# Half-size first weight blocks, zero products ahead of them, and a second load queue at the head of a hybrid decoder kernel

## The chip, the cores and the metric

One Trainium2 chip, one core. The metric is device time in microseconds (us). The kernel's engines are TensorE (PE, with its weight loads PEld), VectorE (DVE), ScalarE (ACT), GpSimd (POOL), and the queue of SyncE (SP) that issues transfers; ACT can issue transfers too.

## The reference

Two layers over 1024 prompt tokens and 8 decode tokens with 1024 features, all in float32. The change touches only the head of layer 0: RMSNorm of the input, then the combined input projection, of which the first part computed is the value projection of the first gated-linear-attention head together with the low-rank gate code.

```
h = rmsnorm(x, norm_g[0])
q, k, v, g, a_low, hb, gate_b, gate_c, z_b = _split(h @ w_in, EVEN_SPLITS)
```

The RMS factor of a token is applied after the product, so the products begin on x times the norm's gain. Everything behind that (the linear attention, the short convolution, the output projection, the convolution module of layer 1, the last norm) is as it was.

## The kernel before

**Number format.** Each float32 operand is cut in two parts: a high part in the fast matmul format (an ACT copy) and a low part, operand minus high part (a DVE or POOL subtraction). A product of two operands is three matmuls: high by high, high by low, low by high. `split_ahead` (L228) cuts the weight blocks (tiles wh and wl from the raw block wr), `split_x` (L295) cuts the input (tile A; ACT at L296, DVE at L297), and it also multiplies by the norm's gain, which stands in the first eight columns of the parameter tile prm.

**Weights.** A list, `plan`, holds the weight blocks in the order of their use. `load_ahead` (L218) issues the transfer of a block into one of two raw buffers, `split_ahead` cuts it. The first two blocks are 128 x 1088 each and hold k = 0 to 3 and k = 4 to 7 of the first value projection.

**Input.** The first 128 tokens come in two tiles xf of four k each, at L307; the other tokens of chunk 0 (256 columns for each of eight k), then chunks 1 and 2, then the first 128 tokens again in the layout needed later, come through `load_x` (L300), 32 transfers in all. All of these, the two weight blocks and prm are issued from SP's queue, in the order weight block, prm, xf, weight block, xf, and then the 32.

**The first products.** `v_proj(0)` (L337) runs over nine token tiles t; for each it runs over k = 0 to 7 with three matmuls each (L351), 216 matmuls of up to 272 columns. Tile t = 0 needs the two xf tiles and both weight blocks; t = 1 and 2 need the rest of chunk 0.

**Order.** ACT's instructions, the transfers it issues among them, stay in the order of the program text (`manual_schedule`). The order on PE, DVE, POOL and SP is set by a planner that plays the program through in simulated time (`schedule_with_timeline_sim`); it also places every semaphore. ACT loads its function table ahead of its first activation. The small tile scT, zeroed on POOL at L330, is later the masked score tile of the attention.

Of the kernel before, what the change touches and what calls it, by code (L numbers as in the profile page):

```python
# [7 lines left out]
F32 = mybir.dt.float32  # L8
F32R = mybir.dt.float32r
I32 = mybir.dt.int32  # L10
AF = mybir.ActivationFunctionType
ALU = mybir.AluOpType
# [3 lines left out]
P = 128  # L16
# [21 lines left out]
NPAR = _o  # L38
# [23 lines left out]
def hybrid_step(ctx, tc, xT, wv, wa, wup, woa, wic, woc, par, ident_d, mask_d, smask_d, sgla, ssc, scc,  # L62
                y_o, glap_o, scp_o, ccp_o, glas_o, scs_o, ccs_o):
    nc = tc.nc
    pe, act, dve, pool, sp = nc.tensor, nc.scalar, nc.vector, nc.gpsimd, nc.sync
# [12 lines left out]
    def nm(s):  # L78
        cnt[0] += 1
        return f"{s}{cnt[0]}"  # L80

    def T(shape, dt=F32, s="t"):
        return ring.tile(shape, dt, tag="t", name=nm(s))
# [4 lines left out]
    def g_t():  # L88
        return gp.tile([P, 512], F32, tag="g", name=nm("g"))
# [8 lines left out]
    prm = const.tile([P, NPAR], F32, tag="prm", name="prm")  # L98
# [7 lines left out]
    def pcol(n, i):  # L106
        return prm[:, PAR[n] + i:PAR[n] + i + 1]
# [84 lines left out]
    raws, parts, used, sums_of = [], [], [0], {}  # L192
# [25 lines left out]
    def load_ahead(i):  # L218
        while len(raws) < min(i, len(plan)):
            _, src, n, e, _ = plan[len(raws)]  # L220
            if src is None:
                raws.append(None)
                continue
            raw = wp.tile([P, 1088], F32, tag="raw", name=nm("wr"), bufs=2)
            sp.dma_start(out=raw[:, :n], in_=src)
            raws.append(raw)

    def split_ahead(i):  # L228
        while len(parts) < min(i, len(plan)):
            load_ahead(len(parts) + 2)  # L230
            key, src, n, e, where = plan[len(parts)]
            raw = raws[len(parts)]
            if key[0] in ("s0", "s1"):
                raw = sums_of[key[1]][key[0] == "s1"]
            if where is ring:
                h, l = T([P, n], F32R, s="wh"), T([P, n], F32R, s="wl")
            else:
                h = wp.tile([P, 1088], F32R, tag="wh", name=nm("wh"))
                l = wp.tile([P, 1088], F32R, tag="wl", name=nm("wl"))
            act.activation(h[:, :n], raw[:, :n], AF.Copy)  # L240
            if isinstance(e, int):
                sp.dma_start(out=l[:, :n].bitcast(F32), in_=wl_d[e])
            else:
                e.tensor_tensor(out=l[:, :n], in0=raw[:, :n], in1=h[:, :n].bitcast(F32), op=ALU.subtract)  # L244
            parts.append((h, l))

    def pair_sums(q):
        if q not in sums_of:
            e0 = next(i for i, p in enumerate(plan) if p[0] == ("w0", q))
            load_ahead(e0 + 2)  # L250
            a, b = raws[e0], raws[e0 + 1]
            s0, s1 = T([P, KT * P], s="s0"), T([P, KT * P], s="s1")
            lo, hi = slice(0, 512), slice(512, 1024)
            dve.tensor_tensor(out=s0[:, lo], in0=b[:, lo], in1=b[:, hi], op=ALU.add)
            dve.tensor_tensor(out=s0[:, hi], in0=s0[:, lo], in1=a[:, lo], op=ALU.subtract)
            dve.tensor_tensor(out=s1[:, lo], in0=a[:, lo], in1=b[:, lo], op=ALU.subtract)
            dve.tensor_tensor(out=s1[:, hi], in0=a[:, hi], in1=s0[:, hi], op=ALU.subtract)
            sums_of[q] = s0, s1

    def W(*key, ahead=2):  # L260
        i = used[0]
        assert plan[i][0] == key, (plan[i][0], key)
        used[0] += 1
        split_ahead(i + 1 + ahead)
        return parts[i]
# [22 lines left out]
            tick()  # L288


    xk = [T([P, NT], s="x") for _ in range(KT)]
    xf = [T([P, 4, P], s="xf") for _ in range(2)]
    A = new_a("A")

    def split_x(c, k, src, lo, hi):  # L295
        act.activation(A[c][:, k, lo:hi], src, AF.Copy, scale=pcol("g0", k))  # L296
        dve.scalar_tensor_tensor(out=A[c][:, KT + k, lo:hi], in0=src, scalar=pcol("g0", k),  # L297
                                 in1=A[c][:, k, lo:hi].bitcast(F32), op0=ALU.mult, op1=ALU.subtract)

    def load_x(k, lo, hi):  # L300
        sp.dma_start(out=xk[k][:, lo:hi], in_=xT[:, k, lo:hi])

    load_ahead(1)
    sp.dma_start(out=prm, in_=par)
    for j in range(2):
        load_ahead(j + 1)
        sp.dma_start(out=xf[j], in_=xT[:, j * 4:j * 4 + 4, 0:P])  # L307
    parts_of = [(0, P, CH[0][1]), (1, 0, CH[1][1]), (2, 0, CH[2][1])]
    for c, lo, hi in parts_of:
        for k in range(KT):  # L310
            load_x(k, CH[c][0] + lo, CH[c][0] + hi)
    for k in range(KT):
        load_x(k, 0, P)
    for j in range(2):
        split_ahead(j + 1)
        for k in range(4):
            split_x(0, j * 4 + k, xf[j][:, k, :], 0, P)

    def split_rest():
        for c, lo, hi in parts_of:  # L320
# [5 lines left out]
    sp.dma_start(out=mask, in_=mask_d)  # L326
    smask = T([P, NT], s="smask")
    sp.dma_start(out=smask, in_=smask_d)
    scT = T([P, 2, 512], s="scT")
    pool.memset(scT, 0.0)  # L330
    al = T([P, 9, RS], s="al")
    pool.memset(al, 0.0)
    alT = T([RS, NT], F32R, s="alT")
# [3 lines left out]
    def v_proj(h):  # L337
        w, width = [W("v", h, j, ahead=2 - j if h else 1 - j) for j in range(2)], VW if h == 0 else DV
        V = [T([P, 4, DV], s="V") for _ in range(2)]
        for t in range(9):  # L340
            ps = mm_t()
            c = min(t // 3, 2)
            lo, m = t * P - CH[c][0], P if t < 8 else ND
            i = 0
            for k in range(KT):
                wh, wl = w[k // 4]
                ks = slice((k % 4) * width, (k % 4 + 1) * width)
                xh = A[c][:, k, lo:lo + m]
                xl = A[c][:, KT + k, lo:lo + m]
                for x, y in ((xh, wh), (xh, wl), (xl, wh)):  # L350
                    pe.matmul(ps[:m, :width], x, y[:, ks], start=(i == 0), stop=(i == 23))  # L351
                    i += 1
            e = act if h == 0 and t < V_ACT else dve
            copy = lambda out, in_: act.activation(out, in_, AF.Copy) if e is act else dve.tensor_copy(out, in_)
            if t < 8:
                copy(V[t // 4][:, t % 4, :], ps[:, :DV])
            else:
                vd = T([ND, DV], s="vd")
                copy(vd, ps[:ND, :DV])
            if h == 0:  # L360
                copy(al[:m, t, 0:RANK], ps[:m, DV:VW])
                if t in W_AT:
                    split_ahead(len(parts) + 1)
            tick()
        start(v_dec(h, vd))
        return V
# [432 lines left out]
    for i in range(KT):  # L799
# [3 lines left out]
        cuts = [slice(lo, lo + n) for lo, n in CH]  # L803
# [62 lines left out]
    for lo, n in CH:  # L866
        s = slice(lo, lo + n)
# [208 lines left out]
    for i in range(KT):  # L1076
# [28 lines left out]
        else:  # L1105
            for b, take in ((8 + i, take_gate), (i, take_u)):
                for c, s, ps in units(W("c", b), X):
# [4 lines left out]
                                 in1=pd[:, i, :], op0=ALU.mult, op1=ALU.add)  # L1112
# [237 lines left out]
```

## Time and profile before

| | us |
|---|---|
| median of three runs | 1295.73 |
| lowest, highest | 1295.63, 1297.95 |
| profiled execution | 1294.83 |
| its span, first to last instruction | 1293.1 |
| PE busy in it | 1257.2 (97%) |
| DVE, POOL, ACT busy | 842.5, 669.6, 578.2 |
| mean granted TensorE clock | 0.99 of full |

The busy times are of one profiled execution. "Idle before" is the time an engine stood still just before an instruction, with what released it. Rows of a timeline merge neighbouring instructions of one line: "x4" is four of them, and the second number is the time from the first one's start to the last one's end.

### The profile page before, as it was taken

The page shows a single profiled execution, that of the slowest core. Times are in us where ns is not written, and L with a number is a line of the kernel's source. Part 1 is how long each engine was busy: PE and PEld are TensorE (multiplying, and loading weights), DVE is VectorE, ACT ScalarE, POOL GpSimd, SP SyncE. Part 2 cuts the span into 40 slices and gives each one's busy share as a digit, 9 for nine tenths or more (in the row PEclk, how much of TensorE's full clock was granted, in tenths as well). Part 3 has the DMA queues.
Part 4 walks back from the last instruction along what each step waited for, and adds up shares of the span by engine and source line. Part 5 has one row for each costly group of instructions (what it writes and reads, how often), then busy time and mean ns, then how long its engine had stood idle before and what let it go on. Part 6 is the DMA issues. An engine that isn't in the chain of part 4 may idle for free.

```text
span 1293.1 us, 20369 instructions
## 1 busy us (share of the span) xinstructions
PE 1257.2 (97%) x8189; PEld 1236.5 (96%) x8189; DVE 842.5 (65%) x1150; ACT 578.2 (45%) x892; POOL 669.6 (52%) x405
## 2 busy tenths in 40 slices
PE   7999999999999999999999999997999999998995
PEld 7999999999999999999999999997999999997995
DVE  6542554445536999999976254216579899989636
ACT  7434616335345523333332233315666929548513
POOL 1455445538375555455645322312298989846313
PEclk9999999999999999999999999999999999999997
DMA  7113032242153432323249998732222323223203
GB/s 260 34 66 135 18 131 103 78 155 99 42 211 130 165 108 72 131 82 131 84 153 349 361 380 304 268 115 85 100 93 99 99 98 103 98 67 134 96 17 131
DMA packets 62542, 174.10 MB, mean 135 GB/s; under 512 B 7776, under 2 KB 25792, under 8 KB 62448
## 3 DMA queue, kind: packets, MB, share of 16 engines
q1 hardware_dynamic: 62176, 172.53, 37.9%
q8 instruction: 64, 1.05, 0.3%
q14 instruction: 30, 0.25, 0.1%
q10 hardware_dynamic: 272, 0.27, 0.1%
HBM read 128.37 MB, written 44.41 MB: 134 GB/s over the span
## 4 chain that ended last, share of the span: by engine, by line
PE 87%; DVE 6%; ACT 3%; POOL 2%; issue 1%; DMA 0%; DVEq 0%; ACTq 0%; POOLq 0%
PE mm L274 61%; PE mm L735 8%; PE mm L351 6%; PE g L735 6%; PE g L274 1%; PE g L552 1%; PE g L513 1%; DVE cv L1159 1%; PE g L579 1%; PE g L582 1%; PE g L514 1%; PE g L392 1%; DVE Y L1253 1%; DVE sqv L1146 0%; ACT L95 0%
## 5 line engine op out<-in xcount | busy, mean ns | idle before, releaser
L274 PE MATMUL mm<-A,wh 128*128 128x384 f32 (+1 forms) x1536 | 245.5, 311 | 0.0
L274 PEld LDWEIGHTS mm<-A,wh 128*128 128x128 f32 x1536 | 231.4, 188 | 0.8
L244 POOL TENSOR_TENSOR wl<-wr,wh 128x1024 fp32r<-128x1024 f32 x51 | 124.5, 2448 | 193.8 <-ACT wh L240 193.8
L274 PE MATMUL mm<-X,wh 128*128 128x384 f32 (+1 forms) x1152 | 195.8, 321 | 6.0 <-ACT wh L240 5.6
L274 PEld LDWEIGHTS mm<-X,wh 128*128 128x128 f32 x1152 | 184.4, 190 | 8.3 <-ACT wh L240 6.0
L240 ACT ACTIVATE wh<-wr 128x1024 fp32r<-128x1024 f32 (+1 forms) x104 | 109.0, 1055 | 139.2 <-PE g L735 51.1
L274 PE MATMUL mm<-A,wl 128*128 128x384 f32 (+1 forms) x768 | 129.6, 310 | 0.0
L274 PEld LDWEIGHTS mm<-A,wl 128*128 128x128 f32 x768 | 117.4, 188 | 0.1
L1027 POOL TENSOR_TENSOR pa<-pa,pr 128x1024 f32<-128x1024 f32 x45 | 110.4, 2454 | 12.8 <-ACT pr L1025 10.4
L351 PE MATMUL mm<-wh,A 128*128 128x256 f32 (+3 forms) x576 | 108.3, 287 | 6.4 <-ACT A L296 6.4
L1013 DVE SCALAR_TENSOR_TENSOR g<-u,late,g 128x512 f32<-128x512 f32 x150 | 102.3, 747 | 1.1 <-ACT g L1010 1.1
L274 PE MATMUL mm<-X,wl 128*128 128x384 f32 (+1 forms) x576 | 102.1, 318 | 0.0
L351 PEld LDWEIGHTS mm<-wh,A 128*128 128x128 f32 (+1 forms) x576 | 86.7, 180 | 8.3 <-ACT A L296 6.4
L274 PEld LDWEIGHTS mm<-X,wl 128*128 128x128 f32 x576 | 92.4, 188 | 0.1
L244 POOL TENSOR_TENSOR wl<-s,wh 128x1024 fp32r<-128x1024 f32 x24 | 67.9, 2840 | 41.1 <-ACT wh L240 41.1
L351 PE MATMUL mm<-wl,A 128*128 128x256 f32 (+3 forms) x288 | 82.2, 286 | 0.1
L274 PE MATMUL mm<-M,wh 128*128 128x384 f32 (+1 forms) x384 | 67.5, 328 | 3.4 <-ACT M L1175 2.3
L274 PEld LDWEIGHTS mm<-M,wh 128*128 128x128 f32 x384 | 63.1, 193 | 4.8 <-ACT M L1175 2.6
L986 DVE SCALAR_TENSOR_TENSOR g<-us,prm,g 128x512 f32<-128x512 f32 x70 | 52.8, 754 | 12.5 <-ACT g L984 10.9
L201 ACT ACTIVATE ph<-pw 128x1024 fp32r<-128x1024 f32 x27 | 28.5, 1057 | 66.9 <-DMA pw<-in_dram 34.0
L913 DVE TENSOR_TENSOR x<-mm,x 128x384 f32<-128x384 f32 (+1 forms) x21 | 10.7, 515 | 71.6 <-PE mm L274 46.4
L1025 ACT ACTIVATE pr<-u,late 128x512 f32<-128x512 f32 x90 | 57.2, 716 | 0.0
(287 smaller groups left out, 2581.5 us busy)
## 6 DMA issues: line engine op xcount, KB each, us to landing
wr<-in_dram SPq DMA_DIRECT2D x102, 512.0 KB, 3.4
pw<-in_dram SPq DMA_DIRECT2D x27, 512.0 KB, 6.8
wl_d<-pw SPq DMA_DIRECT2D x27, 512.0 KB, 5.1
wl<-wl_d SPq DMA_DIRECT2D x27, 512.0 KB, 3.6
b<-y_d SPq DMA_DIRECT2D x14, 516.0 KB, 7.4
bc<-dec_d SPq DMA_DIRECT2D x12, 512.0 KB, 5.0
O<-o_d SPq DMA_DIRECT2D x8, 768.0 KB, 9.9
x<-in_dram SPq DMA_DIRECT2D x8, 516.0 KB, 6.3
```

Of the source, the lines that this page charges most:

```text
L201: act.activation(h, r, AF.Copy)
L240: act.activation(h[:, :n], raw[:, :n], AF.Copy)
L244: e.tensor_tensor(out=l[:, :n], in0=raw[:, :n], in1=h[:, :n].bitcast(F32), op=ALU.subtract)
L274: pe.matmul(out, wl if p == "w" else wh, xl if p == "x" else xh, start=((first or into is None) and i == 0), stop=(part[1] and i == len(se ...
L351: pe.matmul(ps[:m, :width], x, y[:, ks], start=(i == 0), stop=(i == 23))
L392: pe.matmul(ps[:, :n], ones, t, start=(i == 0), stop=(i == len(terms) - 1))
L513: pe.matmul(ps[:, j * P:(j + 1) * P], ke[:, lo:lo + P], qe[:, lo:lo + P], start=True, stop=True)
L735: pe.matmul(out, (l if p == "w" else h)[:, ws], xs[k][p == "x"], start=(i == 0), stop=(i == 11))
L986: dve.scalar_tensor_tensor(out=cm if j == 15 else acc, in0=us[:, j:j + n], scalar=ev(j), in1=acc, op0=ALU.mult, op1=ALU.add)
L1013: dve.scalar_tensor_tensor(out=acc[r], in0=u[:, 1 - r, lo + j:hi + j], scalar=df(r, j), in1=acc[r], op0=ALU.mult, op1=ALU.add)
L1025: act.activation(pr[:, r, :], u[:, 1 - r, lo + j:hi + j], AF.Copy, scale=df(r, j))
L1027: pool.tensor_tensor(out=ac, in0=ac, in1=pr, op=ALU.add)
```

## The change

The first two weight blocks come in two transfers of half the columns each, and are cut in halves: high half, low half, then the two k of x that belong to it. SP issues the first xf tile ahead of the first weight block. prm moves to ACT's queue, in two transfers (its first eight columns, then the rest), and four of the eight transfers of chunk 0's rest (odd k) move to ACT's queue as well. All six stand at the head of ACT's program. scT and its zeroing move ahead, and three products of 256 columns on it go to a spare tile of PSUM that nothing reads.

```
             raw = wp.tile([P, 1088], F32, tag="raw", name=nm("wr"), bufs=2)
-            sp.dma_start(out=raw[:, :n], in_=src)
+            cuts = 2 if len(raws) < 2 else 1
+            for i in range(cuts):
+                cut = slice(i * n // cuts, (i + 1) * n // cuts)
+                sp.dma_start(out=raw[:, cut], in_=src[:, cut])
             raws.append(raw)
...
+            if len(parts) < 2:
+                for i in range(2):
+                    cut = slice(i * n // 2, (i + 1) * n // 2)
+                    act.activation(h[:, cut], raw[:, cut], AF.Copy)
+                    e.tensor_tensor(out=l[:, cut], in0=raw[:, cut], in1=h[:, cut].bitcast(F32), op=ALU.subtract)
+                    for k in range(2):
+                        k += i * 2
+                        split_x(0, len(parts) * 4 + k, xf[len(parts)][:, k, :], 0, P)
+                parts.append((h, l))
+                continue
...
+    scT = T([P, 2, 512], s="scT")
+    pool.memset(scT, 0.0)
+    idle = g_t()
+    for _ in range(3):
+        pe.matmul(idle[:, 0:256], scT[:, 0, 0:P], scT[:, 1, 0:256], start=True, stop=True)
...
     def load_x(k, lo, hi):
-        sp.dma_start(out=xk[k][:, lo:hi], in_=xT[:, k, lo:hi])
-
-    load_ahead(1)
-    sp.dma_start(out=prm, in_=par)
+        (act if lo == P and k % 2 else sp).dma_start(out=xk[k][:, lo:hi], in_=xT[:, k, lo:hi])
+
+    act.dma_start(out=prm[:, 0:8], in_=par[:, 0:8])
+    act.dma_start(out=prm[:, 8:NPAR], in_=par[:, 8:NPAR])
     for j in range(2):
+        sp.dma_start(out=xf[j], in_=xT[:, j * 4:j * 4 + 4, 0:P])
         load_ahead(j + 1)
-        sp.dma_start(out=xf[j], in_=xT[:, j * 4:j * 4 + 4, 0:P])
...
-    for j in range(2):
-        split_ahead(j + 1)
-        for k in range(4):
-            split_x(0, j * 4 + k, xf[j][:, k, :], 0, P)
+    split_ahead(2)
...
-    scT = T([P, 2, 512], s="scT")
-    pool.memset(scT, 0.0)
```

## Rows read from the trace of the kernel before

**Rows 1.** The page's first part: busy time, share of the span, instructions.
```profile
PE 1257.2 (97%) x8189; PEld 1236.5 (96%) x8189; DVE 842.5 (65%) x1150; ACT 578.2 (45%) x892; POOL 669.6 (52%) x405
```
**Rows 2.** PE's waits, whole span: us in total, times, longest.
```profile
PE mm L351 <- ACT A L296: 6.4, 1, 6.4
...
PE mm L274 <- ACT wh L240: 5.6, 1, 5.6
```
**Rows 3.** Windows, PE alone: length, busy (instructions), PEclk, DMA share, GB/s.
```profile
6.35:10.55 4.20, 4.06 (x15) 1.00 1.08 368
10.75:36.00 25.25, 25.25 (x204) 1.00 0.66 215
```
**Rows 4.** PE's timeline, end of the first tile's start: start us, us, line.
```profile
9.32 0.43 PE L351 MATMUL mm<-wl,A 128*128 128x272 f32 x1
9.55 0.65 PE L351 MATMUL mm<-wh,A 128*128 128x272 f32 x2
10.14 0.40 PE L351 MATMUL mm<-wl,A 128*128 128x272 f32 x1
...
10.61 0.29 PE L351 MATMUL mm<-wl,A 128*128 128x272 f32 x1
10.74 0.28 PE L351 MATMUL mm<-wh,A 128*128 128x272 f32 x1
```
**Rows 5.** ACT's timeline from the start, with idle time before and its releaser.
```profile
0.73 1.28 ACT L240 ACT_TABLE_LOAD   x1 [0.73 <-PEq L1328]
4.59 1.11 ACT L240 ACTIVATE wh<-wr 128x1088 fp32r<-128x1088 f32 x1 [2.58 <-DMA wr<-in_dram]
5.90 1.28 ACT L296 ACTIVATE A<-xf,prm 128x128 fp32r<-128x128 f32 x4 [0.20 <-DMA xf<-in_dram]
7.65 1.11 ACT L240 ACTIVATE wh<-wr 128x1088 fp32r<-128x1088 f32 x1 [0.47 <-DMA wr<-in_dram]
8.67 1.26 ACT L296 ACTIVATE A<-xf,prm 128x128 fp32r<-128x128 f32 x4
```
**Rows 6.** DVE's timeline of the same stretch.
```profile
6.94 1.14 DVE L297 SCALAR_TENSOR_TENSOR A<-xf,prm,A 128x128 fp32r<-128x128 f32 x4
8.79 1.29 DVE L244 TENSOR_TENSOR wl<-wr,wh 128x1088 fp32r<-128x1088 f32 x1 [0.71 <-ACT wh L240]
10.00 1.14 DVE L297 SCALAR_TENSOR_TENSOR A<-xf,prm,A 128x128 fp32r<-128x128 f32 x4
```
**Rows 7.** Transfers issued: queue, count, KB each, median us from issue to landing.
```profile
wr<-in_dram SPq DMA_DIRECT2D x2, 544.0 KB, 5.5
x<-in_dram SPq DMA_DIRECT2D x8, 128.0 KB, 5.1
xf<-in_dram SPq DMA_DIRECT2D x2, 256.0 KB
prm<-in_dram SPq DMA_DIRECT2D x1, 181.0 KB, 3.9
```
**Rows 8.** SP's timeline: issue start, length; the eleventh, twelfth and thirteenth transfer.
```profile
5.96 0.44 SPq L301 DMA_DIRECT2D x<-in_dram  x1
...
7.64 0.33 SPq L301 DMA_DIRECT2D x<-in_dram  x1
...
8.40 0.33 SPq L301 DMA_DIRECT2D x<-in_dram  x1
```
**Rows 9.** Windows: length, PE, PEld, DVE, ACT, POOL busy, PEclk, DMA share, GB/s.
```profile
3.00:4.00 1.00, 0.00 (x0) 0.00 (x0) 0.00 (x0) 0.00 (x0) 0.00 (x0) 1.00 0.98 390
...
7.00:8.00 1.00, 0.92 (x4) 0.92 (x5) 1.00 (x5) 0.53 (x2) 0.00 (x0) 1.00 1.09 343
```
**Rows 10.** ACT's queue, the one transfer that ACT issues in the kernel before.
```profile
1288.97 0.42 ACTq L1258 DMA_DIRECT2D out_dram<-Y  x1
```
**Rows 11.** POOL's timeline at the start: the zeroing of scT.
```profile
0.73 0.95 POOL L330 MEMSET scT<- 128x1024 f32 x1 [0.29 <-POOLq L1328]
```
**Rows 12.** The chain of waits: four plain float32 products of 256 columns, two records each.
```profile
106.00 1.73 PE g L552 x8
```

## The prediction, made before the changed kernel was run

> **What bounds the kernel now.** I read the page's busy times first: PE is busy for 97% of the span, no other engine for more than 65% [rows 1]. So the time moves only if PE's work starts earlier, runs faster or loses a gap. PE's waits, longest first, come next: the longest of all is the first one, 6.4 us, in which nothing has been multiplied yet [rows 2], and it is the only one that the change aims at. The stretch behind it shows what a shift there would be worth: from 10.75 to 36 us PE is busy for 25.25 us of 25.25 [rows 3], so whatever the first tile of the value projection gains or loses is passed on whole. What happens before 10.75 is therefore the question.
>
> PE's timeline there shows two things. The matmuls of 272 columns start 0.23 us apart (9.32, 9.55) and later 0.13 apart (10.61, 10.74) [rows 4]: 272 columns at 1.2 and at 2.4 GHz. Up to 10.55 there are 15 of them [rows 3], all at the low level. (The windows' column of the granted clock stays at 1.00 all the while [rows 3, 9]; the spacing is what I go by.) And at 10.14 the queue stands still for a moment: the two records from 9.55 are through at 10.0, and the next product needs the low part of the second weight block, which DVE cuts from 8.79 on, in 1.29 us [rows 4, 6]. So even a fast clock from the start would have met that wait; it would have saved the two slow matmuls behind it, 0.2 us. The chain that sets PE's progress is the second block's: landed at 7.65, ACT's copy, DVE's subtraction at 8.79, PE at 10.14.
>
> As a mark I take the start of the 25th matmul, where tile t = 0 is done: the 16th starts at 10.61 [rows 4], nine later at 0.125 us each is 11.74 us.
>
> **When transfers land.** With the sizes [rows 7] the landings of before lie on a line. The first block (544 KB) released ACT at 4.59. The transfers behind it are prm, xf, block two, xf, in one queue: 981 KB are in when the first xf releases ACT at 5.90, 1525 KB when the second block does at 7.65 [rows 5], and 1781 KB at the second xf. That last landing is read from the queue: SP's eleventh, twelfth and thirteenth transfers are issued at 5.96, 7.64 and 8.40 [rows 8], right behind the landings of the third (5.90) and fourth (7.65), so a transfer is issued only when the eighth before it is in, and the second xf, the fifth, landed at 8.4. From 544 to 1781 KB is 1237 KB in 3.81 us, 325 KB a us. So B KB in are reached at 2.92 + B/325 us; for 981 and 1525 KB this gives 5.94 and 7.61, as read. The 16 transfer engines are full in this time (share 0.98 and 1.09, 390 and 343 GB/s, with one queue) [rows 9].
>
> **Two queues.** Does a second queue bring its bytes beside the first or out of the same rate? With one queue the share stands at 1, so I take the same rate, shared equally while both have work. The trace has no stretch with two queues; the other end of the price is that SP's bytes are not delayed at all.
>
> The Trainium skill's page "DMA: Bandwidth & Descriptors", section "Issuing engines are not separate DMA queues", says that transfers issued from different engines run on the same 16 engines and interleave, and that a second issuer saves only issuing time. By that rule the change's second queue costs the first one bytes, as I take it; no run here shows two queues yet.
>
> **The sum.** SP now sends 256 (xf), 272, 272 (block one), 256, 272, 272 KB. ACT sends 181 KB of prm and 4 x 128 KB of x, 693 KB. In the kernel before, those 512 KB of x came behind everything that t = 0 needs; now they come ahead of its second half. Shared equally, block one's first half is in at 2 x 528 = 1056 KB, 6.17 us; its second half at 800 + 693 = 1493 KB, 7.51; the second xf at 8.30; block two's halves at 2021 and 2293 KB, 9.14 and 9.98, where the whole of it came at 7.65 before.
>
> ACT first issues six transfers at 0.42 us [rows 10], then loads its table, 1.28 us [rows 5]: ready at 0.73 + 2.5 + 1.28 = 4.5. With the eighth-before rule the last of the six may wait for prm (shared, 362 KB, 4.0 us), which makes it 5.7. Both are hidden by the landing at 6.17.
>
> Costs of the pieces, start to start: an ACT copy of 1088 columns 1.02 us (7.65 to 8.67), of 128 columns 0.30 [rows 5]; on a line, 544 columns 0.61. DVE: 1.21 for 1088 (8.79 to 10.00), 0.27 for 128 [rows 6]; 544 columns 0.68. So halves cost ACT 1.22 a block for 1.02, DVE 1.36 for 1.21. From block two's first half at 9.14: ACT's high half to 9.75, two k to 10.35, second high half (landed 9.98) to 10.96. DVE: low half 9.8 to 10.48, two k to 11.02, low half to 11.70, two k to 12.24. PE's last product of t = 0 starts at 12.28, the 25th at 12.41. That is 0.7 us later than 11.74.
>
> The clock does not change this. PE's first product comes at 6.17 + 0.61 + 0.30 + 0.04 = 7.1, and 24 at 0.227 end at 12.6; at the high level DVE sets 12.4. So the three products on zeros are worth 0 to 0.2 us here. They cost nothing: scT is zeroed at 1.68 [rows 11], a product of 256 columns takes 1.73/4 = 0.43 us at the high level [rows 12], twice that at the low, so they are done between 3.0 and 4.3, ahead of any data.
>
> Behind t = 0 nothing new is late: the rest of chunk 0 now lands with its total bytes unchanged (1781 + 8 x 128 = 2805 KB, 11.6 us), and ACT reaches it at 11.6 after its last two k. SP's queue is shorter by three issues, which no engine waits for at that point. So the sum is +0.7: 1295.5 for the profiled execution of 1294.83, and 1295.73 + 0.7 = 1296.4 beside the median, which lies 0.9 above that execution.
>
> **Rivals.**
>
> *The order wins.* If ACT's bytes do not hold up SP's, the landings are 4.54, 5.38, 6.17, 7.01 and 7.84. ACT is ready at 4.5, so block two's first half starts at 7.01: ACT's second high half ends at 8.83, DVE's last two k at 10.10, the 25th matmul starts at 10.27 at the high clock: -1.5, 1294.2. At the low clock PE starts at 5.5 and 24 x 0.227 ends at 10.95: -0.8. For it: the first xf and half a block are 528 KB where before 981 KB had to be in. Against it: the full share in rows 9.
>
> *ACT stands behind its own transfers.* ACT's order is that of the text, and its six transfers come before every activation. A transfer waits for the eighth before it. If the eight are counted in the order of the text over both queues, the last x on ACT waits for block two's second half, 7.84 to 9.98 us, and ACT's first copy starts 1.70 later (issue and table), at 9.5 to 11.7. Nothing is then missing, but ACT and DVE have the whole head to do: DVE 0.65 behind, four steps of 0.68 + 0.54, the 25th matmul at 15.2 to 17.4. That is +3.5 to +5.7, 1300.3 in the middle. It decides from the point at which ACT is held beyond 6.2 us. For it: the rows of SP show such holds. Against it: the two queues issue side by side in the planner's time, and if they are counted alternately the last x waits only for prm. No row shows how two queues are counted.
>
> *The order elsewhere.* The planner sets the order on four engines in simulated time, and scT and a PSUM tile are taken earlier. A different order later on can move the end by some microseconds either way, as the longest waits behind the head are of that size (the largest below the 6.4 is 5.6 us [rows 2]). Half that, 2.8: 1292.9 or 1298.5.
>
> *The change does nothing.* The terms cancel within 0.3: 1295.7. This lies between the first two cases.
>
> **Chances and range.** Forecast, with the cancelling case, 0.52; the order wins 0.24; ACT held 0.12; order elsewhere 0.12, both signs alike. The measurement can tell about 0.2% from no change, 2.6 us: 1293.1 to 1298.3. Faster than that needs the order elsewhere, or a gain beyond what I see: 0.10. Slower: ACT held, and half of the order elsewhere, less what stays inside: 0.16. The rest, 0.74, is within. The range from 1293.4 to 1299.5 holds the first two cases, the low edge of the third and most of the fourth; the likeliest case alone runs from 1295.7 to 1297.2.
>
> **What the profile would show.** The first product at about 7.1 us instead of 6.35, at 0.23 us spacing or 0.13. The second block's first half landing at about 9.1; at 7 the first rival is right. ACT's table load starting near 3.3 to 4.4 and not later; at 8 or later it is held. The matmuls of t = 0 spread with gaps for DVE's halves and the 25th start near 12.4. If PE ends the value projection of head 0 as early as before or earlier, the contention was mis-sized; if the time moves by over 3 us with the head in place, the cause lies elsewhere.

## The result, and the profile after

The changed kernel took 1304.91 us (median of 6 runs, 1303.56 to 1306.63) beside 1295.68 for the kernel before in the same session (6 runs, 1294.95 to 1297.95). The ratio is 1.0070, 95% interval 1.0058 to 1.0081: slower by about 9.1 us, where 1296.4 was forecast with a range up to 1299.5. The profiled executions agree: the span is 1301.8 us for 1293.1.

The busy line has hardly moved [rows 1]; PE is busy 3.4 us longer, 2.9 of them the zero products, and the span is 8.7 us longer. The loss is time in which PE computes none of the kernel's own products. (The profiled execution is the fastest of the six.)

```profile
PE 1260.6 (97%) x8195; PEld 1238.4 (95%) x8195; DVE 843.6 (65%) x1152; ACT 578.5 (44%) x894; POOL 668.9 (51%) x405
```

PE's waits of the first 110 us of the changed kernel (us in total, times, longest). The first answers to the first of [rows 2].

```profile
PE mm L365 <- ACT A L315: 6.8, 1, 6.8
PE mm L287 <- DVE la L510: 2.4, 1, 2.4
PE g L309 <- POOL scT L306: 1.7, 1, 1.7
...
```

ACT's timeline of the changed kernel at the start, the counterpart of [rows 5] (start, length, engine, line; the two rows behind the first "..." are the second and third of the four x transfers, read in windows of their own).

```profile
0.73 0.43 ACTq L322 DMA_DIRECT2D prm<-in_dram  x1
1.20 0.44 ACTq L323 DMA_DIRECT2D prm<-in_dram  x1
3.57 5.52 ACTq L320 DMA_DIRECT2D x<-in_dram  x4
9.12 1.28 ACT L246 ACT_TABLE_LOAD   x1 [9.12 <-DMA x<-in_dram]
10.42 0.66 ACT L246 ACTIVATE wh<-wr 128x544 fp32r<-128x544 f32 x1
...
5.07 0.33 ACTq L320 DMA_DIRECT2D x<-in_dram  x1
...
7.20 0.34 ACTq L320 DMA_DIRECT2D x<-in_dram  x1
...
12.69 5.32 ACT L315 ACTIVATE A<-x,prm 128x256 fp32r<-128x256 f32 x12
17.91 0.65 ACT L246 ACTIVATE wh<-wr 128x544 fp32r<-128x544 f32 x1
```

The four x are issued at 3.57, 5.07, 7.20 and 8.76 (the last 0.33 before 9.09), each held until an earlier transfer lands. ACT's table load, which was at 0.73, comes at 9.12, and its first copy at 10.42 where it was 4.59. The row of 17.91 shows something that I missed in the diff: the new `for i in range(2)` reuses the name of `split_ahead`'s argument, so the loop over blocks ends after the first one, and the second weight block is cut only behind twelve cuts of x.

How late PE is, at the same work, in the kernel before and then in the changed one: the first 256-column product of the second head, the column sums of the squared input, the last of the first three gate products (L458, L472), the first key and query products (L274, L287), the first score products (the changed kernel's fence also has its zero products and its two waits in the query and key products).

```profile
35.93 0.28 PE L351 MATMUL mm<-wl,A 128*128 128x256 f32 x1
...
47.73 1.90 PE L392 MATMUL g<-ss,ones 128*128 128x384 f32 x6
...
61.75 0.29 PE L458 MATMUL g<-alT,wup_r 80*128 80x264 f32 x1
...
65.16 2.96 PE L274 MATMUL mm<-A,wh 128*128 128x384 f32 x16
...
92.36 0.38 PE L513 MATMUL g<-E,tm 128*128 128x128 f32 x2
```

```profile
1.74 2.93 PE L309 MATMUL g<-scT 128*128 128x256 f32 x6 [1.74 <-POOL scT L306]
11.42 0.59 PE L365 MATMUL mm<-wh,A 128*128 128x272 f32 x1 [6.75 <-ACT A L315]
...
40.93 0.28 PE L365 MATMUL mm<-wl,A 128*128 128x256 f32 x1
...
55.63 1.90 PE L406 MATMUL g<-ss,ones 128*128 128x384 f32 x6
...
70.13 0.52 PE L287 MATMUL mm<-A,wh 128*128 128x384 f32 x2
70.49 0.28 PE L472 MATMUL g<-alT,wup_r 80*128 80x264 f32 x1
...
82.75 3.07 PE L287 MATMUL mm<-A,wh 128*128 128x384 f32 x16 [0.86 <-ACT wh L253]
88.19 4.50 PE L287 MATMUL mm<-A,wh 128*128 128x384 f32 x28 [2.36 <-DVE la L510]
...
100.98 0.38 PE L527 MATMUL g<-E,tm 128*128 128x128 f32 x2
```

PE starts 5.07 us later (11.42 for 6.35) and is 5.00 later at the second head (40.93 for 35.93) and still 4.97 later at the first key and query products (70.13 for 65.16). At the score products it is 8.62 later (100.98 for 92.36). So the loss has two terms: 5.0 in the head, and 3.6 between 70 and 101 us, of which two waits, 0.86 and 2.36, make 3.2. From there on it stays: the span ends 8.7 later. The column sums give a hint of the second term: they are 7.9 later while the products around them are 5.0 later, so they stand at another place in PE's order. The last of the first three gate products is 8.7 later (70.49 for 61.75).

### The profile page after: what moved, and what is told of

It reads as the page before. It is cut to its first block, busy times and chain, and to the rows that moved or that the text cites. A ratio compares the mean times of both kernels' runs of the same rounds, so it can differ in the third digit from the quotient of the medians.

```text
span 1301.8 us, 20387 instructions
## 1 busy us (share of the span) xinstructions
PE 1260.6 (97%) x8195; PEld 1238.4 (95%) x8195; DVE 843.6 (65%) x1152; ACT 578.5 (44%) x894; POOL 668.9 (51%) x405
## 4 chain that ended last, share of the span: by engine, by line
PE 85%; DVE 6%; ACT 3%; POOL 2%; issue 1%; DMA 1%; SPq 0%; DVEq 0%; POOLq 0%; ACTq 0%
PE mm L287 59%; PE mm L749 8%; PE mm L365 6%; PE g L749 6%; PE g L287 1%; PE g L566 1%; PE g L527 1%; DVE cv L1173 1%; PE g L593 1%; PE g L596 1%; PE g L528 1%; DMA xa<-in_dram 1%; PE g L406 1%; DVE Y L1267 1%; ACT L95 0%
## 5 line engine op out<-in xcount | busy, mean ns | idle before, releaser
L287 PE MATMUL mm<-A,wh 128*128 128x384 f32 (+1 forms) x1536 | 245.8, 311 | 3.2 <-DVE la L510 2.4
L287 PEld LDWEIGHTS mm<-A,wh 128*128 128x128 f32 x1536 | 231.3, 188 | 4.4 <-DVE la L510 2.7
L287 PE MATMUL mm<-X,wh 128*128 128x384 f32 (+1 forms) x1152 | 195.8, 321 | 5.9 <-ACT wh L253 5.6
L287 PEld LDWEIGHTS mm<-X,wh 128*128 128x128 f32 x1152 | 184.3, 189 | 8.2 <-ACT wh L253 6.0
L253 ACT ACTIVATE wh<-wr 128x1024 fp32r<-128x1024 f32 x102 | 106.8, 1054 | 130.9 <-PE g L749 50.8
L287 PE MATMUL mm<-A,wl 128*128 128x384 f32 (+1 forms) x768 | 129.6, 310 | 0.0
L287 PEld LDWEIGHTS mm<-A,wl 128*128 128x128 f32 x768 | 117.3, 188 | 0.1
L1041 POOL TENSOR_TENSOR pa<-pa,pr 128x1024 f32<-128x1024 f32 x45 | 110.6, 2457 | 12.8 <-ACT pr L1039 10.4
L287 PE MATMUL mm<-X,wl 128*128 128x384 f32 (+1 forms) x576 | 102.1, 318 | 0.0
L287 PEld LDWEIGHTS mm<-X,wl 128*128 128x128 f32 x576 | 92.4, 188 | 0.1
L287 PE MATMUL mm<-M,wh 128*128 128x384 f32 (+1 forms) x384 | 67.4, 327 | 3.4 <-ACT M L1189 2.3
L287 PEld LDWEIGHTS mm<-M,wh 128*128 128x128 f32 x384 | 63.1, 193 | 4.8 <-ACT M L1189 2.6
L287 PE MATMUL mm<-b,wh 128*128 128x384 f32 (+1 forms) x336 | 56.5, 319 | 0.0
## 6 DMA issues: line engine op xcount, KB each, us to landing
O<-o_d SPq DMA_DIRECT2D x8, 768.0 KB, 10.4
```

Of the source, the lines that this page charges most:

```text
L287: pe.matmul(out, wl if p == "w" else wh, xl if p == "x" else xh, start=((first or into is None) and i == 0), stop=(part[1] and i == len(se ...
L1041: pool.tensor_tensor(out=ac, in0=ac, in1=pr, op=ALU.add)
```

## The experiments

Theory at first: ACT's own transfers hold ACT (the head), and everything behind is late by that. Rivals: the second block's late cut by the overwritten name, the halves and the zero products, the contention of two queues. Later rivals for the second term: the late third weight block, and the places that the planner gives to the gate chain. The times:

| kernel | us, median (lowest to highest) | ratio to before, 95% interval |
|---|---|---|
| changed | 1304.91 (1303.56 to 1306.63) | 1.0070 (1.0058 to 1.0081) |
| before + x on ACT | 1305.09 (1304.45 to 1306.32) | 1.0074 (1.0062 to 1.0087) |
| changed, x on SP | 1298.81 (1297.05 to 1300.26) | 1.0022 (1.0013 to 1.0031) |
| changed, own loop names | 1303.70 (1303.17 to 1305.96) | 1.0066 (1.0054 to 1.0079) |
| x on SP and own names | 1299.25 (1298.13 to 1301.06) | 1.0026 (1.0015 to 1.0037) |
| the same, third block early | 1294.81 (1293.47 to 1295.91) | 0.9993 (0.9984 to 1.0002) |
| before, third block early | 1295.71 (1294.63 to 1297.62) | 0.9999 (0.9991 to 1.0008) |
| x on SP, own names, no zeros | 1298.31 (1296.13 to 1299.28) | 1.0018 (1.0009 to 1.0027) |
| third block early, five zeros | 1293.79 (1293.46 to 1296.23) | 0.9990 (0.9981 to 0.9999) |
| changed, own names, third block early | 1304.14 (1303.59 to 1304.39) | 1.0063 (1.0051 to 1.0075) |
| before + x on POOL | 1303.30 (1301.63 to 1304.11) | 1.0054 (1.0042 to 1.0066) |
| changed, gates early | 1306.60 (1306.05 to 1308.32) | 1.0085 (1.0072 to 1.0099) |
| before, gates late | 1299.84 (1298.56 to 1300.90) | 1.0030 (1.0019 to 1.0041) |

**Which part of the change.** Four kernels: the changed one with all x on SP's queue, the changed one with its own loop names, both edits, and the kernel before with nothing but the four odd x on ACT's queue.

```
-        (act if lo == P and k % 2 else sp).dma_start(out=xk[k][:, lo:hi], ...)
+        sp.dma_start(out=xk[k][:, lo:hi], ...)                      # x on SP
-                for i in range(2):
-                    cut = slice(i * n // 2, (i + 1) * n // 2)
+                for p in range(2):                                  # own names
+                    cut = slice(p * n // 2, (p + 1) * n // 2)
```

> The changed kernel with all eight loads of chunk 0's rest back on SP's queue; prm stays on ACT, everything else as changed. Theory A (ACT stands behind its own four loads, each of which waits for the transfer eight before it): table load near 1.7 us instead of 9.1, first half block in at about 5.1, first real product near 6.1 instead of 11.42, and the whole loss goes: 1294.5 to 1297. Theory B (the loss comes from the second weight block being cut only behind twelve cuts of x, as the loop variable i overwrites split_ahead's argument): that order is still here, so 1300 or more. Theory C (the second queue takes the first one's bytes): as A, but the second block's halves would have come no later than before.

> The changed kernel with the loop variables in load_ahead and split_ahead renamed, so that the second block is cut right behind the first; the four loads stay on ACT. Theory A: first product still at 11.4, the time 1303 to 1306. Theory B: the time falls by 3 us or more, to 1297 to 1302.

> Both mended: loads on SP and the second block cut right behind the first. Theory A: within 1 us of the kernel with only the loads on SP, 1294 to 1296.5; head: first product near 6.1, last cut of the first tile on DVE near 10.5. Theory B: 3 us or more below the one with only the loads on SP.

> The kernel before with one edit of the change: the four odd loads of chunk 0's rest on ACT's queue. The planner counts the eight so that the last of them waits for the second xf tile (landed 8.4 before). Theory A: table load not before 8.8, first product 11 to 12 instead of 6.35, time +4.5 to +9: 1300 to 1305. Theories B and C: no second cut order is changed here; C alone (512 KB ahead of the first blocks at equal shares) gives at most +1.5: 1297.

The last of these settles the main part: the four x on ACT, put alone into the kernel before, cost 0.74%, 9.6 us (8.9 between the medians, 1305.09 and 1296.22), as much as the whole change. ACT's timeline and PE's waits of that kernel show the same two places as the changed kernel's; in its profile PE is 6.1 us late at the second head (41.99 for 35.93) and loses 4.5 more between the key and query products and the score products:

```profile
0.73 8.11 ACTq L301 DMA_DIRECT2D x<-in_dram  x4
8.87 1.28 ACT L240 ACT_TABLE_LOAD   x1 [8.87 <-DMA x<-in_dram]
```

```profile
PE mm L351 <- ACT A L296: 11.6, 1, 11.6
PE mm L274 <- DVE la L496: 2.4, 1, 2.4
...
```

With x back on SP the table load is at 1.66 and the first product at 6.29, and 6 us of the loss go. The loop names by themselves change nothing that can be told (1303.70 and 1304.91, intervals overlap): PE has tiles t = 1 and 2 to fill the time until the second block is cut. With x on SP the late cut does show in the trace, though not in the time: with the old names PE reaches the second head at 37.80 us, with own names at 35.98, but it then waits 0.6 us for POOL's wl with the old names and 2.1 with its own.

But with x on SP 0.22 to 0.26%, about 3 us, stay unexplained by that. In the kernel with both edits the head is as before (first product 6.33, second head 35.98), and the loss comes later. POOL's timeline, PE's wait and the windows of that kernel (length, PE, PEld, DVE, ACT, POOL busy, PEclk, DMA share, GB/s):

```profile
39.85 4.67 POOL L257 TENSOR_TENSOR wl<-wr,wh 128x1024 fp32r<-128x1024 f32 x2
```

```profile
42.25 0.58 PE L365 MATMUL mm<-wl,A 128*128 128x256 f32 x1 [2.09 <-POOL wl L257]
```

```profile
42.00:44.00 2.00, 1.75 (x8) 1.75 (x9) 0.00 (x0) 0.00 (x0) 2.00 (x2) 0.55 0.33 121
44.00:46.00 2.00, 2.00 (x13) 2.00 (x13) 0.42 (x1) 0.00 (x0) 2.00 (x2) 0.60 0.61 199
```

In the kernel before, the same subtraction starts at 38.32 and is through at 40.7; the first product that needs it stands 42 places behind the second head's first, at about 35.93 + 42 x 0.117 = 40.8, so PE just doesn't wait. Here it starts 1.5 us later, because SP issues the third weight block, behind all the x, at 22.43 for 21.49, ACT's copy of it comes at 27.28 for 25.72, and POOL takes it in that order. And the product stands 13 places earlier, as I counted in PE's instructions as built, 1.5 us. The wait of 2.09 us is followed by almost 4 us at a granted clock of 0.55 to 0.60: from 42.25 to 46 us 19 products start where 32 would at 0.117 us each, 1.5 us more.

**The third block, and the zero products.** The call that fetches it is moved ahead of the last eight x, in that kernel and in the kernel before; a third kernel has no zero products, a fourth has five.

```
+    split_ahead(2)
     for k in range(KT):
         load_x(k, 0, P)
-    split_ahead(2)
```

> The twice mended kernel (loads on SP, second block cut right behind the first) with one move: the third weight block (first half of the second value projection) is issued ahead of the last eight 64 KB loads of x. Theory D (the 3 us that stay after both repairs come from that block landing 1.6 us later, which delays the chain ACT copy, eight squares, POOL low half of the fourth block, and PE runs out of it at 40 to 42 us, waits 2.1 us and falls to the low clock): the block releases ACT by 25.5 instead of 27.28, the wait for POOL's wl goes, 1294.5 to 1296.5. Theory E (the 3 us are the planner's other order, or the cost of cutting in halves): 1298 to 1300.

> The kernel before with the same move alone. Theory D: PE had no wait for that chain there, so nothing to win at the wait itself: 1295 to 1296.5, at best 1 us below the kernel before where the chain was only just in time. Theory E: the order changes by itself, 2 us or more either way.

> The twice mended kernel without the three products on zeros. If they help: slower by the low-clock time they save, up to 1.5 us. If they only move the low-clock stretch (the granted clock fell to 0.50 at 8 to 11.4 us behind the pause from 4.7 to 6.3): within 0.5 us of the twice mended kernel, 1298.7 to 1299.8, with about the same number of matmuls at the 0.227 us spacing.

> The kernel with both repairs and the third block's earlier issue, with five products on zeros instead of three, so that PE is busy from 1.74 until about the first real product at 6.33. If the pause behind the zeros is what costs the clock: no stretch at 0.227 us spacing behind 6.4, the first value projection over 1 to 1.5 us earlier than in the one with three (35.0 to 34.5), and the time 0 to 1.5 us lower, as far as the chain of ACT and POOL is early enough. If not: the same within 0.5 us, or up to 0.5 slower where the zeros run past 6.33.

With the block issued at 16.78 POOL's subtraction starts at 35.28, PE's only waits up to 110 us are the two at the head, and the loss goes: 1294.81, which can't be told from the kernel before. In the kernel before the same move gives nothing (0.9999), as it should, since nothing waited there. So in the kernel with both edits the residue was this wait and the low clock behind it, shown from both sides.

Without zeros the kernel with the late third block takes 1298.31, with three 1299.25, measured in two sessions; the intervals overlap, so no worth of the three zeros can be told. PE reaches the second head at 36.11 without them and at 35.98 with them. With five it is 35.35, for 36.08 with three (both with the early third block). PE's timeline of the kernel with five, and the windows of the kernel with three and of the one with five:

```profile
1.74 4.63 PE L309 MATMUL g<-scT 128*128 128x256 f32 x10 [1.74 <-POOL scT L306]
5.94 0.66 PE L365 MATMUL mm<-wh,A 128*128 128x272 f32 x1
...
7.77 0.29 PE L365 MATMUL mm<-wl,A 128*128 128x272 f32 x1
7.90 0.45 PE L365 MATMUL mm<-wh,A 128*128 128x272 f32 x2
```

```profile
8.00:9.00 1.00, 1.00 (x5) 0.92 (x6) 0.90 (x3) 1.00 (x4) 0.00 (x0) 0.69 1.10 383
9.00:10.00 1.00, 1.00 (x5) 0.90 (x5) 1.00 (x4) 1.00 (x3) 0.00 (x0) 0.50 1.04 353
```

```profile
8.00:9.00 1.00, 0.86 (x6) 0.56 (x5) 0.61 (x2) 1.00 (x4) 0.00 (x0) 1.00 1.10 381
9.00:10.00 1.00, 0.92 (x6) 0.72 (x6) 1.00 (x4) 1.00 (x3) 0.00 (x0) 1.00 1.09 365
```

With three, PE is idle from 4.67 to about 6.2 and the granted clock falls to 0.50 some 2 us after it has begun again; with five there is no pause and it stays at 1.00. The column alone would not do as evidence here: without zeros it stands at 1.00 from 6 to 11 us as well, while the products are 0.23 us apart, as in [rows 3, 4]. With five they are 0.13 apart from 7.77 on, up to the first gap at 8.4, and no longer run of them 0.23 apart follows. Five differ from three in the pause and in two more products, and no run parts the two. The time is 1293.79, below the kernel before by 1.7 us between the medians (0.9990, interval up to 0.9999), at the edge of what can be measured; against three zeros (1294.81) the intervals overlap, so there the 0.7 us at the second head is all that is shown. It is the fastest version by its median.

**The second term of the loss.** Two kernels: the changed one with its own names and the early third block, x still on ACT; and the kernel before with the four odd x on POOL's queue, so that two queues run and ACT issues nothing.

```
-        sp.dma_start(out=xk[k][:, lo:hi], in_=xT[:, k, lo:hi])
+        (pool if lo == P and k % 2 else sp).dma_start(out=xk[k][:, lo:hi], ...)
```

> The changed kernel with its own loop variables, the four x still issued by ACT, and the third weight block fetched ahead of the last eight x. It tells whether the loss has two separate terms. Two terms: ACT stays held until about 9 us, the first real product stays at 11.4 to 11.5 and the second head's value projection at about 41 (+5.0 against the kernel before), but the third block is in early, the wait for DVE's la at 97 to 100 us goes, and the end comes at +5.0 with the 1.7 to 2 us that the same move gains elsewhere taken or not: 1299 to 1301. One term: the late second stretch comes from ACT being 5 us late with everything, so moving the block changes nothing and the time stays at 1303.5 to 1304.5.

> The kernel before, with only the four odd x issued by POOL's queue, so that a second queue has 512 KB of its own from the start and ACT issues none. It measures the forecast's contention term by itself. Shared rate (the forecast): the first block lands between 4.6 and 6.2 us (4.59 before), the second at about 2.92 + (1525 + 512)/325 = 9.2 (7.65 before), the first tile's last products come about 1.5 us later and the time goes to 1296.5 to 1297.5. SP's bytes first: the landings stay at 4.6 and 7.65 and the time within 0.5 us of the kernel before. Held: POOL's transfers wait for SP's, and POOL's first subtraction or memset is late as ACT's copy was; the product column shows a wait for POOL.

The first missed: 1304.14, and the wait for DVE's la is there as before (2.4), with the third block issued at 17.35. ACT, late itself, copies that block at 26.49, hardly earlier than without the move (26.68 with own names), so this kernel alone does not clear the block. The kernel with only x on ACT does: there the copy comes at 25.68, as in the kernel before (25.72), and the wait is there all the same. The late third block is not the second term. The second kernel missed in the other direction: 1303.30, 6 us above what was expected of shared landings. ACT's timeline of it and PE's:

```profile
4.61 1.11 ACT L240 ACTIVATE wh<-wr 128x1088 fp32r<-128x1088 f32 x1 [2.58 <-DMA wr<-in_dram]
6.80 1.28 ACT L296 ACTIVATE A<-xf,prm 128x128 fp32r<-128x128 f32 x4 [1.09 <-DMA xf<-in_dram]
8.97 1.11 ACT L240 ACTIVATE wh<-wr 128x1088 fp32r<-128x1088 f32 x1 [0.89 <-DMA wr<-in_dram]
```

```profile
39.17 0.28 PE L351 MATMUL mm<-wl,A 128*128 128x256 f32 x1
...
53.89 1.90 PE L392 MATMUL g<-ss,ones 128*128 128x384 f32 x6
...
86.49 5.72 PE L274 MATMUL mm<-A,wh 128*128 128x384 f32 x25 [2.39 <-DVE la L496]
```

The landings of xf and of the second block are as the forecast had them for a shared rate: xf at 6.80 for 5.90, the second block at 8.97 for 7.65, where 9.2 was expected. The first block lost nothing (4.61 for 4.59). On the line of the prediction 8.97 us is (8.97 - 2.92) x 325 = 1966 KB, its own 1525 and 441 of POOL's 512. On PE the same 1.32 us show at the product that waits for the second block's low part (11.46 for 10.14), but at the second head it is 3.2 us late (39.17 for 35.93): its products stay 0.23 us apart until 15.7, where before they were 0.13 apart from 10.6 on. POOL issues its four x from 1.27 to 3.57 us without a hold. But then PE again waits 2.39 us for DVE's la, though ACT was never held and the third block was early (ACT's copy at 23.81 for 25.72). What this kernel shares with the others is the distance from the second head to the column sums: 53.89 - 39.17 = 14.7 us, in the changed kernel 55.63 - 40.93 = 14.7, in the kernel before 47.73 - 35.93 = 11.8. So I counted PE's instructions as built, the first being 0:

| kernel | place of the column sums | of the first three gate products | first key and query product |
|---|---|---|---|
| before | 315 to 317 | 404, 408, 420 | 449 |
| before, third block early | 315 to 317 | 404, 408, 420 | 449 |
| before + x on ACT | 338 to 340 | 430, 434, 446 | 449 |
| before + x on POOL | 339 to 341 | 431, 435, 450 | 448 |
| changed (three zeros are in the count) | 342 to 344 | 434, 438, 453 | 451 |
| changed, x on SP (the same) | 318 to 320 | 407, 411, 423 | 452 |

Whenever the four x stand on a second queue, whichever it is, the planner puts the column sums 23 to 24 products later and the last gate product 26 to 30 later. At 0.117 us a product that is 2.8 and 3.0 to 3.5 us. The gate chain then ends after PE has run out of work that doesn't need it. From the last of these three gate products to the first product that waits for DVE's la it is 17.7 us in the changed kernel (70.49 to 88.19), in the one with x on ACT (70.89 to 88.62) and in the one with x on POOL (68.78 to 86.49). In the kernel before 17.7 us behind that gate product is 79.5, and PE doesn't wait.

**The places alone.** Two constants say at which step the RMS factor and the first gates enter the program. Turned one way in the kernel before, they give its order the later places, with no other change; turned the other way in the changed kernel, they give it the earlier ones.

```
-RMS_AT, RMS_WAIT, GATES_AT = 3, 7, 4
+RMS_AT, RMS_WAIT, GATES_AT = 3, 9, 6      # before, gates late
+RMS_AT, RMS_WAIT, GATES_AT = 3, 4, 6      # changed, gates early
```

> The kernel before, with nothing of the change, and the two constants turned the other way (wait 9 for 7, step 6 for 4): the column sums stand at place 338 to 340 of PE's order (315 to 317), the first gate products at 429, 436 and 441 (404, 408, 420), as the four x on a second queue put them (338 to 340; 430, 434, 446). Head, loads and weights are those of the kernel before. Order theory: PE waits some 2.4 us for DVE's la near 90 us, the first score products come 3 to 5 us later and the time is 1298.5 to 1300.5. If places in the order are not what costs, the time stays within 0.5 us of the kernel before.

> The changed kernel as it is, with two constants that say at which step the input's RMS factor and the first gates are put into the program (wait 4 for 7, step 6 for 4). In PE's planned order the column sums of the squares then stand at place 315 to 317 (315 to 317 in the kernel before, 342 to 344 in the changed one) and the first three gate products at 401 to 403 (404, 408, 420; 434, 438, 453). ACT's hold at the head stays. Order theory: the 3.6 us lost between 70 and 92 us are these 27 to 33 places, so the wait for DVE's la goes and the time comes to 1296 + 5.0 = 1300 to 1301.5. Data theory: the gate chain is late because its inputs are, so PE then waits for the column sums or the gates instead and the time stays at 1303.5 to 1305.

The first is as the order theory has it: 1299.84, 0.30% more (interval 0.19 to 0.41), with the head of the kernel before but for 0.5 us (36.41 for 35.93). PE's timeline:

```profile
36.41 0.28 PE L351 MATMUL mm<-wl,A 128*128 128x256 f32 x1
...
51.16 1.90 PE L392 MATMUL g<-ss,ones 128*128 128x384 f32 x6
...
64.95 0.28 PE L458 MATMUL g<-alT,wup_r 80*128 80x264 f32 x1
...
82.68 5.99 PE L274 MATMUL mm<-A,wh 128*128 128x384 f32 x28 [2.19 <-DVE la L496]
```

The distance to the column sums is 14.75 us, and the wait for DVE's la is there, 2.19, again 17.7 us behind the gate product. So the places alone, with one load queue and nothing late at the head, make the wait. That the size agrees as well (31.1 us from the first key and query product to the first score product, 30.9 in the changed kernel, 27.2 in the kernel before) is in part chance: in the changed kernel it is the waits of 0.86 and 2.36 with the clock at 1.00 behind them (without the first the second would only be longer, as it ends 17.7 us behind the gate product), here one wait of 2.19 and a granted clock near 0.50 behind it, at which 28 products take 5.99 us instead of 4.50. The other kernel missed: 1306.60, slower than the changed one. Its waits show why. The wait for la is gone, but la itself is ready no earlier (DVE starts on it at 88.3 us, 87.6 in the changed kernel): PE comes to it later. For the constants also put the transposes of the gate code (L455) right behind the column sums, ahead of the RMS factor that their buffers wait for:

```profile
56.32 0.83 PE L455 MATMUL g<-ident,al 128*80 128x128 f32 x3 [2.13 <-DVE rs L399]
58.59 1.45 PE L455 MATMUL g<-ident,al 128*80 128x128 f32 x6 [1.43 <-DVE rs L399]
```

Those 3.6 us, and a granted clock of 0.53 to 0.61 from 56 to 64 us behind them, took the place of what was won. So it neither supports nor contradicts the count.

## Why the prediction was wrong, point by point

**ACT's own transfers.** "Both are hidden by the landing at 6.17" is the step that failed. The forecast had ACT ready at 4.5, or 5.7 if the last x waits for prm; it was ready at 9.1 + 1.28 = 10.4. The rival with ACT held, given 0.12, is what happened, by its own count: eight transfers over both queues, the last x behind block two's second half, ACT's first copy between 9.5 and 11.7 (10.42). That SP counts ACT's transfers too is in SP's waits of the changed kernel, where an x on SP waits for prm, which ACT issued:

```profile
SPq L320 <- DMA prm<-in_dram: 0.4, 1, 0.4
```

I had the rows for such holds on SP [rows 8] and set them aside on the argument that the queues might be counted alternately, which no row bore out. The mark that I named for it, a table load at 8 or later, was met. Its price, 3.5 to 5.7 us, held for the head: 5.0. The way there was another: I let DVE's halves set the pace of the first tile, and the rows have nearly all of it in the first product already (5.07).

**"Behind t = 0 nothing new is late"** failed as well. In the changed kernel the gate chain is late by its place in the order, 3.6 us more. (That the places suffice is shown in the kernel before, with gates late; for the changed kernel it is inferred from the same places and the same 17.7 us.) That is the third rival, "the order elsewhere", which I had priced at 2.8, half of the longest later wait; before with gates late shows 3.9 by the ratio. I had counted the rivals as either-or, and two of them came together: 5.0 + 3.6 = 8.6 of the 8.7 us in the span. What the first tile loses "is passed on whole", as the text says; but the edit also moved work that stands 40 to 60 us behind it.

**The contention** was sized about right in landings, and it was not what decided. In the kernel with x on POOL's queue the second block lands 1.32 us later, close to the forecast's line. That the two queues share equally while both have work is not borne out: the first block came in as before. And the price on PE was too small in that kernel, 3.2 us at the second head: the late block kept the products 0.23 us apart for longer, while the forecast had said that the clock does not change its sum. The Trainium skill's page "DMA: Bandwidth & Descriptors", section "Issuing engines are not separate DMA queues", says that such transfers interleave on the same engines. 441 of the 512 KB went in ahead, so the trace agrees. In the changed kernel the x were themselves held, and the last x, which waits for block two's second half, was issued at 8.76: everything that t = 0 needs was in before ACT's first copy at 10.42.

**The zeros** were worth 0, as forecast. The reason was not quite mine: I took the clock to be covered by DVE's chain, and in the kernel with both edits and the early third block the granted clock falls to 0.50 behind the pause, so that what the three zeros gave is lost again. In the changed kernel it stood at 0.50 before the first product came.

**What was not seen.** The overwritten name costs no time that these runs can tell. That the third weight block has next to no slack in the kernel before (40.7 for 40.8) was not looked for; with x on SP and own names it costs some 4 us, and in the changed kernel, where PE is 5 us late itself, PE does not wait for it. "SP's queue is shorter by three issues, which no engine waits for" was argued from the count of issues alone.

**Still open.** Why the planner places the column sums later when four x stand on another queue: my reading is that it takes the first products to come earlier and the gate chain not, but no run here shows its times. Why the same wait for la lowered the clock in some kernels and not in others is open too. And whether gates placed as before in the changed kernel would give 1300 is not shown, since the one attempt moved the transposes too.

## What to carry to other kernels

A transfer put on a compute engine's queue is an instruction of that engine: if its issue can wait, everything behind it in that engine's program waits too, so count the eighth transfer before it over SP's and ACT's queues together (here POOL's four were not held), and put it behind the engine's first work or leave it on the queue that computes nothing (only the second was run here). When a planner orders the engines, moving a load can move work that is tens of microseconds away: compare the places in the order before believing a sum made at the head. And ask of each load that is pushed back what slack its first user has; here 1.5 us on a load and 13 places in the order made some 4 us.

## What the runs showed of the hardware

A short wait can cost more than its length, but need not. After a wait of 2.09 us PE ran at a granted clock of 0.55 to 0.60 until 46 us, 19 products in the time of 32, 1.5 us more. The same wait for DVE's la, 2.2 to 2.4 us, was followed by a clock near 0.50 with x on ACT, with x on POOL, with gates late and with own names alone (28 products in 5.99 to 6.07 us in three of them), and by a clock of 1.00 in the changed kernel and in the one with own names and the early third block (28 in 4.50 and 4.52). After the pause of about 1.5 us behind three zero products the clock was still 1.00 until 8 us and then fell to 0.69 and 0.50, while PE was busy all the time. In the changed kernel it had fallen to 0.50 by the time that the first product came, and it was back at 1.00 behind the sixteenth:

```profile
9.00:10.00 1.00, 0.00 (x0) 0.00 (x0) 0.00 (x0) 0.88 (x1) 0.00 (x0) 0.50 0.98 306
...
11.40:15.30 3.90, 3.88 (x16) 3.70 (x17) 3.90 (x11) 3.90 (x11) 0.00 (x0) 0.50 0.93 284
15.30:24.00 8.70, 8.70 (x70) 8.62 (x69) 5.82 (x14) 5.31 (x14) 0.00 (x0) 1.00 0.83 242
```
